# Last output projection's rest as a stream beside the first FFN pair, temporaries' pools swapped, down-weight sums pinned in order, second operand stream reordered

## The chip, the cores and the metric

The kernel runs on one core of a Trainium2 chip. The metric is the device time of one execution in microseconds (us). The engines are PE (TensorE, matrix products), DVE (VectorE), ACT (ScalarE), POOL (GpSimd) and SP (SyncE, which here issues the transfers between HBM and on-chip memory). Each engine works off its own list of instructions in order and waits on semaphores for the others. PE writes its results into PSUM banks; DVE and ACT read them from there.

## The reference

One transformer-like block on a sequence of 2048 tokens of width 1024, in float32. A mixer (attention and mLSTM side by side, then an output projection) adds to the residual stream, and a gated FFN follows. The end of the mixer and the FFN are what matters here:

```python
    mix = merged @ w_out[l]
    x = x + gate_m[:, None, :] * rms_norm(mix, g_post_mix[l])

    h2 = modulate(rms_norm(x, g_pre_ffn[l]), shift_f, scale_f)
    ff = (jax.nn.silu(h2 @ w_ffn_gate[l]) * (h2 @ w_ffn_up[l])) @ w_ffn_down[l]
    x = x + gate_f[:, None, :] * rms_norm(ff, g_post_ffn[l])
```

The FFN's inner width is 2816 = 22 x 128.

## The kernel before

**Products.** A float32 factor is split into a high part (ACT, CAST) and a low part (DVE, the factor less its high part), and a product is three matmuls: high by high, high by low, low by high. Every large matmul is 128x128 by 128x512. In the FFN the split is `split_unit` (L1127 ACT, L1128 DVE), and its tile `hl` lies in a ring of four.

**The mixer** runs over four blocks of 512 tokens. Each block ends with `residual_out` (L514): the output projection in two column halves, four accumulators each. For each of the four token groups of the second half it takes the sum of squares (L524), multiplies by the gate (L526), forms the inverse root (L530, L471, POOL's power L474), scales the first half (L540), loads 2 x 512 columns of the residual x (L553), adds (L538 on DVE, L541 on POOL), stores the new residual (L542) and takes its sum of squares for the FFN's norm (L543, L544). Temporaries `tx` come from a ring of six in the pool `tpool`; `mpool` holds `tm` and the gate vector `gg_m`. Both pools are closed at the end of the mixer, and the FFN's pool `fpool` takes their space.

**The FFN** runs over two token blocks of 1024 (`gate_up(0)`, `down(0)`, `gate_up(1)`, `down(1)`). All three weight products use a Strassen-Winograd scheme: a 2x2 block product as seven products (`PROD`). The weight side of five of them needs sums of weight quarters on DVE (L1295, L1296, L1302). The activation side are seven operands, named 11, 21, T2, T4, T1, T3, 22, that `h_combine` builds: for each of four k-steps it loads four pieces of the residual (L1219), scales them (L1224), transposes them on PE (L210, 4 at a time into a PSUM bank), shifts and scales (L1232), subtracts (L1245, L1255, L1256, L1268) and splits. For the first token block it runs as a stream during the mixer and keeps its results in HBM (`STAGED`, `hc_d`), fetched with L1201; for the second it writes straight into the operand tiles (`PLACED`) while `down(0)` runs.

`gate_up` works through 11 pairs of 256 inner columns. A pair is seven gate products and seven up products of 12 matmuls, four products prepared ahead; `combine` adds them up (L1342 to L1356), the gated results go to HBM (`as_d`), and a_sums (L1395 to L1398) makes four more operands. In `gate_up(0)` each pair also loads its down weights (L1375, into one of nine `big` buffers), makes four sums of them on DVE (L1379 to L1382) and stores them (`ws_d`, L1384). `down` runs the seven products over 11 slices each; at the end of a token group its output is normed (L1463, L1465, L1470), multiplied and added to the residual (L1477) and stored (L1478).

**What sets the order.** The code writes the work down with a clock of estimated matmul times: streams (generators) are due at a time and `tick` steps those that are due between products. In the FFN's runner `run2`, `tick` is called only inside products with `weave` set (those of `down` whose result goes to the "X" bank, 0, 2, 4, 6). After that a scheduler of the framework may move instructions on their engines by its own timing; `tc.keep_in_program_order` forbids this for an instruction.

## Time and profile before

| | |
|---|---|
| median of 3 runs | 2816.28 us (2815.49 to 2817.65) |
| the profiled execution | 2815.8 us; its profile spans 2814.1 us |
| PE busy | 2712.0 us, 96% of the span |
| DVE, ACT, POOL busy | 1936.5, 1241.2, 237.0 us |
| moved by transfers | 417.32 MB |
| last matmul of the mixer, first of the FFN | 1461.3 us from the span's start |
| last product of `down(0)` | 2098.4 to 2140.35 us |
| first pair of `gate_up(1)` | from 2144.4 us |

Times in a profile are microseconds from the span's start, durations of one instruction us or ns as said; "[0.34 <-DMA raw]" at a row's end says that the engine had been idle for 0.34 us before the instruction and what ended it. The granted clock is the share of full speed that PE was given. Buffer numbers are left out there (`hl`, `big`); in rows of the instruction order they stand (`hl_13043`). The views the prediction uses are shown there.

### The profile page before, as it was taken

To read this page: it belongs to the slowest core of one execution; us is meant where nothing else is said; L and a number is where in the kernel's file an instruction comes from. 1 tells how busy PE (TensorE), PEld (TensorE's weight loads), DVE (VectorE), ACT (ScalarE), POOL (GpSimd) and SP (SyncE) were. 2 spreads that over 40 slices of the span, in tenths; PEclk is the share of its full clock that TensorE was granted. 3 is DMA by queue.
4 is the path that set the end of the run, shared out by engine and by line. 5 is a ranking of instruction groups with operands and counts; after the bars stand their busy time and mean duration, and the time that the engine had idled before them with its cause. 6 is when DMAs were issued, how large, how long until landed. Compare 5 with 4: busy or idle time off the path is not lost. (4 is left out here: it accounts for less than half of the span.)

```text
span 2814.1 us, 35152 instructions
## 1 busy us (share of the span) xinstructions
PE 2712.0 (96%) x12654; PEld 2206.6 (78%) x12654; DVE 1936.5 (69%) x3780; ACT 1241.2 (44%) x2278; POOL 237.0 (8%) x255
## 2 busy tenths in 40 slices
PE   6999999999999999999987999999997999999997
PEld 4778888788777888778866888888775888888886
DVE  7768667686776976757647866665668666666556
ACT  4543365433655446554433333334554333333443
POOL 3100120011210112100120000000001000000000
PEclk8999999999999999999998999999998999999999
DMA  7233353243534435334578533235666233234567
GB/s 229 90 109 101 100 180 121 83 132 109 186 118 136 133 126 192 105 116 109 210 264 294 194 107 109 98 105 184 204 204 209 92 110 108 96 108 143 179 201 241
DMA packets 282102, 417.32 MB, mean 148 GB/s; under 512 B 18996, under 2 KB 176312, under 8 KB 280136
## 3 DMA queue, kind: packets, MB, share of 16 engines
q1 hardware_dynamic: 281928, 415.08, 45.5%
q8 instruction: 99, 1.62, 0.2%
q14 instruction: 75, 0.61, 0.1%
HBM read 331.11 MB, written 83.92 MB: 147 GB/s over the span
## 5 line engine op out<-in xcount | busy, mean ns | idle before, releaser
L1127 ACT CAST hl<-raw 128x512 fp32r<-128x512 f32 x528 | 314.6, 621 | 388.9 <-PE mix L205 181.8
L1128 DVE TENSOR_TENSOR hl<-raw,hl 128x512 fp32r<-128x512 f32 x528 | 351.5, 687 | 178.8 <-ACT hl L1127 176.4
L260 ACT CAST whi<-raw 128x1024 fp32r<-128x1024 f32 (+1 forms) x208 | 212.1, 1020 | 412.2 <-PE acc L205 355.5
L261 DVE TENSOR_TENSOR wlo<-raw,whi 128x1024 fp32r<-128x1024 f32 (+1 forms) x208 | 251.7, 1211 | 165.2 <-ACT whi L260 164.6
L205 PE MATMUL acc<-hhi,wlo 128*128 128x512 f32 x896 | 354.2, 395 | 0.0
L205 PE MATMUL acc<-hlo,whi 128*128 128x512 f32 x896 | 352.3, 393 | 0.0
L205 PE MATMUL acc<-hhi,whi 128*128 128x512 f32 x896 | 352.2, 393 | 0.0
L205 PE MATMUL acc<-hl,hl 128*128 128x512 f32 x1056 | 249.7, 394 | 12.9 <-DVE hl L1128 10.9
L205 PE MATMUL acc<-big,hl 128*128 128x512 f32 x1056 | 253.6, 389 | 0.0
L205 PEld LDWEIGHTS acc<-hl,hl 128*128 128x128 f32 x1056 | 197.2, 189 | 60.9 <-DVE hl L1128 17.7
L205 PEld LDWEIGHTS acc<-big,hl 128*128 128x128 f32 x1056 | 198.2, 188 | 41.2
L205 PEld LDWEIGHTS acc<-hlo,whi 128*128 128x128 f32 x896 | 168.3, 188 | 38.7 <-issue 4.1
L205 PEld LDWEIGHTS acc<-hhi,wlo 128*128 128x128 f32 x896 | 168.4, 188 | 37.7 <-issue 3.2
L205 PEld LDWEIGHTS acc<-hhi,whi 128*128 128x128 f32 x896 | 168.4, 188 | 37.5 <-issue 4.1
L205 PE MATMUL mix<-big,hl 128*128 128x512 f32 x704 | 196.6, 391 | 0.3 <-DVE hl L1128 0.3
L205 PE MATMUL mix<-hl,hl 128*128 128x512 f32 x792 | 181.6, 390 | 0.0
L205 PEld LDWEIGHTS mix<-hl,hl 128*128 128x128 f32 x792 | 148.1, 188 | 32.8 <-ACT hl L1127 2.2
L205 PE MATMUL acc<-whi,big 128*128 128x512 f32 x512 | 165.3, 395 | 0.0
L205 PE MATMUL acc<-big,whi 128*128 128x512 f32 x512 | 158.2, 393 | 0.0
L474 POOL TENSOR_TENSOR rs<-ms,nhalf 128x1 f32<-128x1 f32 (+1 forms) x40 | 31.4, 789 | 1471.2 <-DVE ms L471 1433.1
L205 PEld LDWEIGHTS mix<-big,hl 128*128 128x128 f32 x704 | 132.5, 188 | 28.3 <-DVE hl L1128 0.7
L205 PE MATMUL acc<-whi,hhi 128*128 128x512 f32 (+1 forms) x384 | 131.4, 369 | 12.7 <-ACT hhi L506 6.3
(301 smaller groups left out, 4983.4 us busy)
## 6 DMA issues: line engine op xcount, KB each, us to landing
raw<-in_w_in_dram SPq DMA_DIRECT2D x76, 1024.0 KB, 5.3
as_d<-w SPq DMA_DIRECT2D x154, 256.0 KB, 2.1
raw<-as_d SPq DMA_DIRECT2D x70, 512.0 KB, 3.6
raw<-in_w_ffn_gate_dram SPq DMA_DIRECT2D x22, 1024.0 KB, 5.7
raw<-in_w_ffn_up_dram SPq DMA_DIRECT2D x22, 1024.0 KB, 5.3
raw<-ws_d SPq DMA_DIRECT2D x40, 512.0 KB, 5.0
tx<-in_w_ada_dram SPq DMA_DIRECT2D x64, 256.0 KB, 3.6
raw<-in_w_out_dram SPq DMA_DIRECT2D x16, 1024.0 KB, 5.0
```

What stands on the lines that cost most here:

```text
L205: T.matmul(o, lhsT=lhsT, rhs=rhs, start=start, stop=stop, skip_group_check=resumed)
L260: A.copy(hv, src)
L261: eng.tensor_tensor(lv, src, hv.bitcast(F32), op=ALU.subtract)
L474: G.tensor_tensor(r[:, :n], ms[:, :n], nhalf[:, :n], op=ALU.pow)
L1127: A.copy(v(hi), src)
L1128: V.tensor_tensor(v(lo), src, v(hi).bitcast(F32), op=ALU.subtract)
```

## The change

Five things are edited.

1. **The rest of the last output projection becomes four streams.** For block 3 `residual_out` gets a list `late`: the first norm steps stay, the second half's product is kept in a further `big` tile (`keep2`), and scale, load of x, add, store and sum of squares (`norm_and_add`) become generators, started by `open_ffn` and stepped beside the first FFN pair. They load x into the FFN's tiles `w`. The fetch of operand (T3, 0) moves from before the output projection to `rest_of_hc`. The first pair's down weights are loaded only after these streams are finished.
2. **`mpool` and `tpool` change places**, and the FFN's pool gives out a `w` tile before `gg_f`, so that the first `w` tiles lie where `tm` was, not `tx`.
3. **The down weights' load and four sums are kept in program order.**
4. **`h_combine` is written anew**: one load ahead, a fixed order of the four quarters, all four transposed before the differences are formed; steps that take a PSUM bank (`yield gap, True`) run only where `weave` is set, while `tick` is now called in every product of the FFN. For the first token block it starts in block 2 with a gap of 8500 (was: at the end of block 1 plus 20000, gap 9500); for the second its gap is 3000 (was 3800), and it is no longer finished as a whole at the end of `down(0)`: before each of the first gate products of `gate_up(1)` `placed` steps it until that product's operand is complete.
5. A product (`Part`) has a hook `before` for that.

```diff
```diff
@@ -81,8 +81,8 @@
     ps_mix = ctx.enter_context(tc.tile_pool(name="ps_mix", bufs=4, space=PSUM))
+    mpool = p1.enter_context(tc.tile_pool(name="mpool", bufs=1))
     tpool = p1.enter_context(tc.tile_pool(name="tpool", bufs=1))
-    mpool = p1.enter_context(tc.tile_pool(name="mpool", bufs=1))
     opool = ctx.enter_context(tc.tile_pool(name="opool", bufs=1, side="right"))
@@ -210,20 +210,22 @@
     def spawn(gen, delay=0.0):
-        st = [now[0] + delay, gen, False]
+        st = [now[0] + delay, gen, False, False]
         streams.append(st)
...
         try:
-            st[0] = now[0] + next(st[1])
+            r = next(st[1])
+            r, st[3] = r if isinstance(r, tuple) else (r, False)
+            st[0] = now[0] + r
         except StopIteration:
...
-    def tick():
+    def tick(banks=True):
         while True:
-            due = [st for st in streams if st[0] <= now[0]]
+            due = [st for st in streams if st[0] <= now[0] and (banks or not st[3])]
             if not due:
@@ -511,7 +513,7 @@
-    def residual_out(nk, lhs, w, keep, resid, gg, dst, t0):
+    def residual_out(nk, lhs, w, keep, resid, gg, dst, t0, late=None):
@@ -522,10 +524,21 @@
             A.activation(junk, ps, AF.Square, accum_out=ss[:, hf * 4 + t:hf * 4 + t + 1])
-            y = st["keep"][:, t, :] if hf == 0 else tx([P, 512])
+            if late is not None and hf and not t:
+                st["keep2"] = keep([NT, 512])
+            y = st["keep"][:, t, :] if hf == 0 else tx([P, 512]) if late is None else st["keep2"][:, t, :]
             V.tensor_tensor(y, ps, gg[:, hf * 512:(hf + 1) * 512], op=ALU.mult)
...
                 return
+            rest = norm_and_add(t, y)
+            if late is None:
+                for _ in rest:
+                    pass
+            else:
+                late.append(rest)
+
+        def norm_and_add(t, y):
+            ss = st["ss"]
             s = small.tile([P, 1], F32, tag="ss1", name=nm("ss1"), bufs=4)
@@ -533,6 +546,7 @@
                 xr = resid(t, c)
+                yield 4000.0
                 y0 = y if h2 else st["keep"][:, t, :]
@@ -540,6 +554,7 @@
                 nc.sync.dma_start(dst[t * P:(t + 1) * P, c], xr)
+                yield 2000.0
                 A.activation(y0, xr, AF.Square, accum_out=sx[:, h2:h2 + 1])
@@ -549,7 +564,7 @@
         def rows(t, c):
-            xr = tx([P, 512])
+            xr = unit() if "pool" in F else tx([P, 512])
             nc.sync.dma_start(xr, src[t * P:(t + 1) * P, c])
@@ -708,6 +723,8 @@
         yield carry
+        if b == 2:
+            yield lambda: F.update(hc=spawn(h_combine(0, STAGED, 8500.0)))
@@ -1076,17 +1093,16 @@
                 R_ada.append(spawn(ada_stream([(5, "gate")], 12000.0)))
-                R["hc"] = spawn(h_combine(0, STAGED, 9500.0), 20000.0)
-                F["hc"] = R["hc"]
             if b + 1 < NBLK:
...
         if b + 1 == NBLK:
-            yield lambda: [fetch(n_, i_) for n_, i_ in (("T4", 1), ("T1", 0), ("T1", 1), ("T3", 0))]
+            yield lambda: [fetch(n_, i_) for n_, i_ in (("T4", 1), ("T1", 0), ("T1", 1))]
         last = list(residual_out(KD, lambda kk, t: tuple(R[m, kk // 4][:, kk % 4, t * P:(t + 1) * P] for m in ("mh", "ml")),
-                                 a["w_out"][0], big, load_rows(x_d[b * TB:(b + 1) * TB, :]), gg_m, x1[b], b * NT))
+                                 a["w_out"][0], big, load_rows(x_d[b * TB:(b + 1) * TB, :]), gg_m, x1[b], b * NT,
+                                 F["rest"] if b + 1 == NBLK else None))
         yield from last[:-1]
@@ -1109,7 +1125,7 @@
     HC = {}
-    F = {}
+    F = {"rest": []}
     as_d = [tc.dram_tile([P, 7, NP, TB], F32, name=f"as_d{i}") for i in range(NB2)]
@@ -1132,6 +1148,7 @@
             self.raw, self.prep, self.mms, self.weave = raw, prep, mms, weave
+            self.before = lambda: None
             raw.left += 1
@@ -1166,9 +1183,9 @@
             advance()
+            it.before()
             for _ in it.mms(made.pop(done)):
-                if it.weave:
-                    tick()
+                tick(it.weave)
             done += 1
@@ -1211,6 +1228,7 @@
                 split_unit(v, hc_part(name, 0)[:, k, :], hc_part(name, 1)[:, k, :])
+                F["put"].add((name, k))
@@ -1232,46 +1250,45 @@
+        QUADS = ((0, 0), (0, 1), (1, 0), (1, 1))
+        order = [(k, half, i) for k in range(4) for half, i in QUADS]
+        x_ = load(*order[0])
+        yield gap
         for k in range(4):
             q = {}
...
+            for half, i in QUADS:
                 scaled(x_, i)
+                yield gap, True
+                q[f"{half + 1}{i + 1}"] = turned(x_, k, half)
+                if (half, i) != (1, 1):
+                    x_ = load(*order[order.index((k, half, i)) + 1])
+                    yield gap
+            t1 = ob()
+            V.tensor_tensor(t1, q["12"], q["11"], op=ALU.subtract)
+            yield gap
+            put("11", k, q.pop("11"))
+            V.tensor_tensor(q["12"], q["22"], q["12"], op=ALU.subtract)
+            yield gap
             t2 = ob()
+            V.tensor_tensor(t2, q["22"], t1, op=ALU.subtract)
+            put("21", k, q["21"])
             yield gap
+            V.tensor_tensor(q["21"], q["21"], t2, op=ALU.subtract)
+            put("T2", k, t2)
             yield gap
+            put("T4", k, q.pop("21"))
+            if k < 3:
+                x_ = load(k + 1, 0, 0)
             yield gap
+            put("T1", k, t1)
             yield gap
             put("T3", k, q.pop("12"))
             yield gap
             put("22", k, q.pop("22"))
             yield gap
     def rest_of_hc():
+        for n_, i_ in (("T3", 0), ("T3", 1), ("22", 0), ("22", 1)):
             fetch(n_, i_)
@@ -1371,15 +1388,15 @@
         def load():
+            if not p:
+                finish(F["rest"])
             st["raw"] = big([2, D])
-            nc.sync.dma_start(st["raw"], wdn[p * 256:(p + 1) * 256, :].rearrange("(k p) c -> p k c", p=P))
+            tc.keep_in_program_order(nc.sync.dma_start(st["raw"], wdn[p * 256:(p + 1) * 256, :].rearrange("(k p) c -> p k c", p=P)))
...
             q = {f"{k + 1}{h + 1}": st["raw"][:, k, h * TB:(h + 1) * TB] for k in range(2) for h in range(2)}
-            V.tensor_tensor(q["11"], q["12"], q["11"], op=ALU.subtract)
-            V.tensor_tensor(q["12"], q["22"], q["12"], op=ALU.subtract)
-            V.tensor_tensor(q["22"], q["22"], q["11"], op=ALU.subtract)
-            V.tensor_tensor(q["21"], q["21"], q["22"], op=ALU.subtract)
+            for o, x, y in (("11", "12", "11"), ("12", "22", "12"), ("22", "22", "11"), ("21", "21", "22")):
+                tc.keep_in_program_order(V.tensor_tensor(q[o], q[x], q[y], op=ALU.subtract))
             for i, n in enumerate(("11", "22", "12", "21")):
@@ -1415,6 +1432,9 @@
             gp, up = list(pair_parts(wg, p, done_g)), list(pair_parts(wu, p, done_u))
+            if b2 and p == 0:
+                for i, pt in enumerate(gp):
+                    pt.before = lambda i=i: placed(PROD[i][1])
             load, sums = down_weights(p)
@@ -1505,7 +1525,8 @@
             def next_h():
-                F["hp"] = spawn(h_combine(b2 + 1, PLACED, 3800.0), 4000.0)
+                F["put"] = set()
+                F["hp"] = spawn(h_combine(b2 + 1, PLACED, 3000.0))
@@ -1514,14 +1535,20 @@
                     yield make(raw, i, p0 + j, j)
-        if not last:
-            yield lambda: finish([F["hp"]])
+
+    def placed(name):
+        st = F["hp"]
+        while (name, 3) not in F["put"]:
+            now[0] = max(now[0], st[0])
+            step(st)
...
         F["pool"] = ctx.enter_context(tc.tile_pool(name="fpool", bufs=1, reuse_waits="tile"))
+        unit()
         F["gg"] = F["pool"].tile([P, D], F32, name="gg_f")
         nc.sync.dma_start(F["gg"], gg_f_d)
+        F["rest"] = [spawn(r, 1000.0 + i * 4000.0) for i, r in enumerate(F["rest"])]
...
         for i, ch in enumerate(ADA):
```
```

Line numbers rise in the changed file (the split is L1143 and L1144, the weight sums L1312, L1313, L1319, the residual's add L552 and L555, the down weights L1394, L1399, L1401).

**PE at the start of the FFN.** `hc` are operands 11 and 21, hcT2h and hcT4h the high parts of T2 and T4; the first row is the first FFN product after the mixer's last matmul. Before:

```order
L205 MATMUL mix_13150<-hc_12573,hl_12978 128x512 x11
L205 MATMUL acc_13132<-hc_12572,hl_12975 128x512 x12
L205 MATMUL mix_13150<-hc_12573,hl_12978 128x512
L205 MATMUL acc_13132<-hcT2h,hl_13126 128x512
L205 MATMUL acc_13132<-hcT2l,hl_13126 128x512
L205 MATMUL mix_13191<-hcT4h,hl_13129 128x512
```

In the change:

```order
L205 MATMUL mix_13073<-hc_12577,hl_12980 128x512 x11
L205 MATMUL acc_13046<-hc_12576,hl_12977 128x512 x12
L205 MATMUL mix_13073<-hc_12577,hl_12980 128x512
L205 MATMUL mix_13126<-hcT4h,hl_13043 128x512
L205 MATMUL mix_13126<-big_12751,hl_13043 128x512
L205 MATMUL mix_13126<-hcT4h,hl_13043 128x512 x2
```

The product with T4, whose weight side is a plain quarter (hl_13043), now stands ahead of that with T2, whose weight side is a sum; both still follow the first 24 matmuls.

**DVE at the same place.** `raw` are the gate weights, hl_13126 (before) and hl_13040 (change) the low part that the T2 product needs. Before, from the end of the residual's rest:

```order
L544 TENSOR_TENSOR sx_13093<-sx_13093 128x1
L471 TENSOR_SCALAR ms_13106<-sx_13093 128x1
L1379 TENSOR_TENSOR big_13502<-big_13502 128x512
L1380 TENSOR_TENSOR big_13502<-big_13502 128x512
L1295 TENSOR_TENSOR w_13122<-raw_12971 128x512
L1381 TENSOR_TENSOR big_13502<-big_13502 128x512
L1296 TENSOR_TENSOR w_13123<-w_13122,raw_12971 128x512
L1302 TENSOR_TENSOR raw_12971<-raw_12971 128x4x128
L1382 TENSOR_TENSOR big_13502<-big_13502 128x512
L1344 TENSOR_TENSOR w_13145<-mix_13150,w_13145 128x512
L1302 TENSOR_TENSOR raw_12971<-raw_12971,w_13123 128x4x128
L1128 TENSOR_TENSOR hl_13126<-w_13123,hl_13126 128x512
```

In the change, from the last accumulator of the output projection:

```order
L530 TENSOR_TENSOR big_12991<-acc_12892,gg_m 128x512
L543 TENSOR_TENSOR ss_13163<-ss_12853 128x1
L1312 TENSOR_TENSOR w_13036<-raw_12973 128x512
L473 TENSOR_SCALAR ms_13165<-ss_13163 128x1
L1313 TENSOR_TENSOR w_13037<-w_13036,raw_12973 128x512
L1319 TENSOR_TENSOR raw_12973<-raw_12973 128x4x128
L1319 TENSOR_TENSOR raw_12973<-raw_12973,w_13037 128x4x128
L1144 TENSOR_TENSOR hl_13040<-w_13037,hl_13040 128x512
L1144 TENSOR_TENSOR hl_13043<-raw_12973,hl_13043 128x512
```

The residual's adds and the sums of a second set of down weights (big_13502) no longer stand ahead of the weight sums; the adds (L552) come 11 rows or more after these rows.

**SP's queue at the start of the FFN.** Before, from the fourth load of x:

```order
L553 DMA tx_13036<-in_x_dram 128x512
L1201 DMA big_13120<-hc_d 128x2048
L1375 DMA big_13208<-in_w_ffn_down_dram 128x2x1024
L542 DMA x_3_194<-tx_12998 128x512
L542 DMA x_3_194<-tx_13004 128x512
L542 DMA x_3_194<-tx_13036 128x512
L553 DMA tx_13062<-in_x_dram 128x512
L542 DMA x_3_194<-tx_13030 128x512
```

In the change, from the load of the FFN's gate vector on (raw_13124 are the second pair's gate weights):

```order
L1550 DMA gg_f<-gg_f_d 128x1024
L568 DMA w_13060<-in_x_dram 128x512
L568 DMA w_13093<-in_x_dram 128x512
L1382 DMA raw_13124<-in_w_ffn_gate_dram 128x8x256
L568 DMA w_13131<-in_x_dram 128x512
L568 DMA w_13143<-in_x_dram 128x512
L568 DMA w_13159<-in_x_dram 128x512
```

The loads of x go into `w` tiles and have the second pair's gate weights among them. The down weights, of which before four sets are loaded ahead of the second pair's gate weights, come after all stores of the residual, and from there one load and one group of four stores per pair.

**PE at the start of `gate_up(1)`.** `ident,ob` are the transposes of `h_combine`. Before, from the end of `down(0)`:

```order
L210 MATMUL mix_18267<-ident,ob_18262 128x128 x4
L205 MATMUL acc_18338<-hc_12572,hl_18100 128x512 x9
L210 MATMUL mix_18282<-ident,ob_18279 128x128 x4
L205 MATMUL acc_18338<-hc_12572,hl_18100 128x512 x3
L210 MATMUL mix_18292<-ident,ob_18289 128x128 x4
L205 MATMUL acc_18338<-hcT2h,hl_18129 128x512
```

In the change, from the last rows of `down(0)` (hl_18216):

```order
L205 MATMUL acc_16372<-hl_18216,hl_18213 128x512 x2
L205 MATMUL mix_18354<-hc_12577,hl_18224 128x512 x12
L205 MATMUL mix_18399<-hcT4h,hl_18330 128x512
L205 MATMUL mix_18399<-big_12751,hl_18330 128x512
L205 MATMUL acc_18333<-hc_12576,hl_18221 128x512 x12
L205 MATMUL mix_18399<-hcT4h,hl_18330 128x512 x2
L205 MATMUL mix_18399<-big_12751,hl_18330 128x512
```

Before, five of `h_combine`'s 16 groups of four transposes stand here and five in the last product of `down(0)`; in the change four stand in the last product and none here, the other twelve (before: six) in products 0, 2 and 4 of `down(0)`. The first gate products follow the last down product directly.

More of the change, by code (lines that the diff above doesn't have):

```diff
@@ L1233, in turned @@
             return q
+        QUADS = ((0, 0), (0, 1), (1, 0), (1, 1))
+        order = [(k, half, i) for k in range(4) for half, i in QUADS]
+        x_ = load(*order[0])
+        yield gap
         for k in range(4):
             q = {}
-            for half, i, name in ((0, 0, "11"), (0, 1, "12")):
-                x_ = load(k, half, i)
-                yield gap
+            for half, i in QUADS:
                 scaled(x_, i)
-                yield gap
-                q[name] = turned(x_, k, half)
-                yield gap
+                yield gap, True
[9 more added lines that the diff above has]
+            yield gap
             t2 = ob()
-            V.tensor_tensor(t2, q["12"], q["11"], op=ALU.subtract)
-            put("11", k, q.pop("11"))
+            V.tensor_tensor(t2, q["22"], t1, op=ALU.subtract)
+            put("21", k, q["21"])
             yield gap
-            put("T1", k, t2)
-            x_ = load(k, 1, 1)
+            V.tensor_tensor(q["21"], q["21"], t2, op=ALU.subtract)
+            put("T2", k, t2)
             yield gap
-            scaled(x_, 1)
+            put("T4", k, q.pop("21"))
+            if k < 3:
+                x_ = load(k + 1, 0, 0)
             yield gap
-            q["22"] = turned(x_, k, 1)
+            put("T1", k, t1)
             yield gap
-            V.tensor_tensor(t2, q["22"], t2, op=ALU.subtract)
-            V.tensor_tensor(q["12"], q["22"], q["12"], op=ALU.subtract)
             put("T3", k, q.pop("12"))
@@ L1259, in h_combine @@
             put("22", k, q.pop("22"))
-            x_ = load(k, 1, 0)
-            yield gap
-            scaled(x_, 0)
-            put("T2", k, t2)
-            yield gap
-            q21 = turned(x_, k, 1)
-            yield gap
-            put("21", k, q21)
-            V.tensor_tensor(t2, q21, t2, op=ALU.subtract)
-            yield gap
-            put("T4", k, t2)
             yield gap
     def rest_of_hc():
-        for n_, i_ in (("T3", 1), ("22", 0), ("22", 1)):
+        for n_, i_ in (("T3", 0), ("T3", 1), ("22", 0), ("22", 1)):
             fetch(n_, i_)
```

1 line of the change is left out of this document (removed).

## The prediction

> **What bounds the kernel now.** I read the page first (busy shares, then the forty slices), then PE's waits, then busy windows over the stretches where a slice falls short, and last the timeline inside them.
>
> ```profile
> PE 2712.0 (96%) x12654; PEld 2206.6 (78%) x12654; DVE 1936.5 (69%) x3780; ACT 1241.2 (44%) x2278; POOL 237.0 (8%) x255
> PE   6999999999999999999987999999997999999997
> PEclk8999999999999999999998999999998999999999
> ```
>
> PE sets the time: a slice is 70 us, and all are full but the first, the last, and those around 1480 and 2140, where the clock falls too. The change touches just these two inner places: A, from the mixer into the FFN, and B, from `down(0)` into `gate_up(1)`. Windows of the large matmuls alone (length, busy, count, granted clock, transfer share, GB/s):
>
> ```profile
> 1461.31:1560.00 98.69, 71.38 (x296) 0.86 0.91 305
> 1560.00:1900.00 340.00, 340.00 (x1501) 1.00 0.34 114
> 1915.00:2098.00 183.00, 179.65 (x783) 1.00 0.60 198
> 2098.44:2140.35 41.91, 32.98 (x133) 1.00 0.81 267
> 2140.35:2174.94 34.59, 16.69 (x42) 0.65 0.50 171
> 2200.00:2560.00 360.00, 360.00 (x1590) 1.00 0.32 104
> ```
>
> The last row is PE at its best: 360 / 1590 = 0.2265 us a matmul. By that price A (first row) holds 296 x 0.2265 = 67.0 us of work in 98.7: **31.6 us lost**. B is two rows: 133 matmuls, 30.1 us, in 41.9 (11.8 lost, the last product of `down(0)`), and 42, 9.5 us, in 34.6 (25.1 lost, the first pair): **36.9 us lost**. These losses hold idle time, slow clock and, in B, transposes. No more than 68.5 us can be won here.
>
> **A, step by step.**
>
> ```profile
> PE acc L205 <- ACT hl L1127: 23.5, 1, 23.5
> ...
> 1490.42 0.80 PE L205 MATMUL acc<-hcT2h,hl 128*128 128x512 f32 x1 [23.51 <-ACT hl L1127]
> ...
> 1482.42 0.15 DVE L471 TENSOR_SCALAR ms<-sx 128x1 f32<-128x1 f32 x1
> 1486.49 0.69 DVE L1379 TENSOR_TENSOR big<-big 128x512 f32<-128x512 f32 x1 [3.92 <-DMA big<-in_w_ffn_down_dram]
> 1487.83 0.68 DVE L1295 TENSOR_TENSOR w<-raw 128x512 f32<-128x512 f32 x1
> 1488.43 0.69 DVE L1381 TENSOR_TENSOR big<-big 128x512 f32<-128x512 f32 x1
> 1489.03 0.69 DVE L1296 TENSOR_TENSOR w<-w,raw 128x512 f32<-128x512 f32 x1
> ...
> 1489.75 0.62 ACT L1127 CAST hl<-w 128x512 fp32r<-128x512 f32 x1 [7.09 <-DVE w L1296]
> ```
>
> PE does the 24 matmuls of operands 11 and 21 and then stands 23.5 us, from 1466.9, for the cast of the T2 product's weight sum. The sum (L1295, L1296) is late because DVE does it in order behind the residual's rest (to 1482.4) and behind down weights (L1379) that landed at 1486.5. In the change's order neither stands ahead of it: the rest are streams whose adds follow 11 rows later, the down weights are pinned behind them. The pools' swap lets the sum write a `w` tile with no transfer to wait for.
>
> What is left, from t = 1461.31, goes by these durations (DVE instructions of 512 columns start 0.60 apart, see above):
>
> ```profile
> 1464.31 0.60 ACT L524 ACTIVATE tx<-acc 128x512 f32<-128x512 f32 x1
> 1464.81 0.19 ACT L524 ACTIVATION_READ_ACCUMULATOR tx<-acc 128x1 f32 x1
> 1465.83 0.72 ACT L540 ACTIVATE big<-big,rs 128x512 f32<-128x512 f32 x1 [0.84 <-POOL rs L474]
> ...
> 1465.26 0.54 POOL L474 TENSOR_TENSOR rs<-ms,nhalf 128x1 f32<-128x1 f32 x1
> ```
>
> - The last accumulator is done at 0.3 (a matmul shows 0.39 us). On ACT: its sum of squares to 1.1, two scalings to 2.6, the third after DVE's product and small steps (2.9) and POOL's power (3.7, with hand-overs of 0.1 to 0.2) to 4.4, then the casts for T2 and T4 to 5.6; DVE's two low parts to 6.3. PE comes for T4 at 24 x 0.2265 = 5.4 and for its low part 0.5 later: 0.7 us lost.
> - SP loads two of the eight x tiles, then the second pair's gate weights, which wait for the seventh split of the first; that split's ring place is free only after the T2 product, at about 11.6. So six x loads go out from about 13.4, and the adds that need them start on DVE behind the split for up's second product, which waits for a ring place freed by the T1 product (17.1). From there to the low part of up's T4 factor DVE has 16 full instructions, 10 us: 28.3. PE wants it at about 25.7: 2.6 us lost.
>
> That is 3.3 us. On top comes POOL, whose four adds now run beside a full DVE:
>
> ```profile
> 1473.93 1.26 POOL L541 TENSOR_TENSOR tx<-big,tx 128x512 f32<-128x512 f32 x1 [3.76 <-DMA tx<-in_x_dram]
> ...
> 1473.97 1.23 DVE L530 TENSOR_TENSOR ss<-ss 128x1 f32<-128x1 f32 x1
> ...
> 1482.22 0.16 DVE L544 TENSOR_TENSOR sx<-sx 128x1 f32<-128x1 f32 x1 [0.85 <-ACT tx L543]
> ```
>
> A one-column DVE add takes 0.16 us, but 1.23 beside POOL's add: up to 1.1 us for each, 4.4 for four. DVE has waits in this stretch that can take some, so I take 2.7. **A leaves 6.0, wins 25.6.** Bounds: 2 us left if the x tiles are early and POOL falls into waits; 13 if POOL costs its 4.4 and the x loads come later by the landing of 1 MB of weights (5.4 us, rows under B).
>
> The Trainium skill, "SBUF — State Buffer", section "SBUF: two separate sides", says that VectorE with two SBUF inputs and GpSimd take one shared port pair by turns and for a whole instruction. The row of 1.23 us agrees. By that rule the eight powers would count like the adds; it speaks against the change and is the first rival below.
>
> **B, step by step.**
>
> ```profile
> 2098.44:2140.35 41.91, 35.12 (x153) 26.28 (x152) 40.18 (x73) 26.73 (x54) 4.92 (x4) 1.00 0.81 267
> 2099.47 0.60 PE L210 MATMUL mix<-ident,ob 128*128 128x128 f32 x4
> 2125.58 2.73 DVE L1477 SCALAR_TENSOR_TENSOR w<-w,rs,w 128x512 f32<-128x512 f32 x4
> 2133.77 0.38 SPq L1365 DMA_DIRECT2D raw<-in_w_ffn_gate_dram  x1
> 2139.18 0.69 DVE L1295 TENSOR_TENSOR w<-raw 128x512 f32<-128x512 f32 x1 [0.34 <-DMA raw<-in_w_ffn_gate_dram]
> 2144.42 3.31 PE L205 MATMUL acc<-hc,hl 128*128 128x512 f32 x9 [2.29 <-DVE w L1465]
> ```
>
> In the last product DVE is busy 40.2 of 41.9 us (fourth number of the first row), with the splits, the outputs of half the tokens and `h_combine`'s third and fourth step. In the change's order DVE has 67 rows from the product's first additions to its last split: 51 full ones at 0.60, 8 output adds at 0.65 (the x4 row), 8 one-column ones at about 0.1 = 36.6 us; seven `h_combine` rows fewer than before. Starting 2 us before the product, DVE ends at 34.6, and PE's last 8 matmuls need 1.8 more: 36.4 instead of 41.9.
>
> Then the first pair. Its gate weights load once the split before last frees a raw tile, at about 31.2 on that clock, and land 5.4 later (2133.77 to 2139.18) at 36.6. Two casts, 38.1; DVE's lows and sums of that quarter, 39.9; PE's first 12 matmuls end at 42.2. After that I find no wait above 0.5: accumulators are free by 41, the operands of `h_combine` are complete. So 144 matmuls, 32.6 us, end at 42.2: **B leaves 9.6 and wins 27.3**. Off that go the six transposing groups that move into `down(0)`, whose PE is full (third row of the windows): 6 x 0.60 = 3.6. `h_combine` is also denser there (12 groups where 6 were); its steps may be waited for. Of the 5.7 us that stretch now loses (183 less 783 x 0.2265), transposes are 6 x 0.6 = 3.6 and 2.1 is waits for six groups; for six more I take 3. **B wins 20.7.** Bounds of what it leaves and adds: 10 (DVE hides more) to 26 (the output's rows keep holding PE as in 2140 to 2145, and each new group waits 1 us).
>
> **What costs nothing, and its cover.** The down weights' sums: four DVE instructions a pair, 2.4 us, and four stores. A pair of PE lasts 168 x 0.2265 = 38 us, and without them DVE is 69% busy with PE full:
>
> ```profile
> 2200.00:2560.00 360.00, 360.00 (x1590) 298.10 (x1589) 247.22 (x399) 130.12 (x226) 0.00 (x0) 1.00 0.32 104
> ```
>
> So DVE goes to 75%. Uncovered they would cost 11 x 2.4 = 26 us. The earlier start of the staged `h_combine` moves rows in the mixer; there PE loses little, all of it in three places:
>
> ```profile
> 400.00:440.00 40.00, 37.66 (x218) 32.79 (x217) 30.90 (x77) 22.13 (x50) 8.85 (x12) 1.00 0.74 232
> 760.00:800.00 40.00, 36.80 (x208) 32.05 (x207) 31.11 (x88) 20.76 (x43) 7.65 (x10) 0.96 0.69 217
> 1120.00:1180.00 60.00, 57.15 (x339) 48.03 (x338) 42.15 (x112) 33.99 (x79) 8.70 (x11) 1.00 0.34 110
> ```
>
> 2.3, 3.2 and 2.9 us idle. I take no change, with 4 us either way (half of the 8.4).
>
> **Sum.** 2814.1 - 25.6 - 20.7 = 2767.8 us of span. The profiled execution lies 1.7 above its span, and the median of the runs shown 0.5 above that execution: 2767.8 + 2.2 = **2770 us**.
>
> **Rivals.**
> 1. *POOL holds DVE in the first pair for each of its instructions.* Four adds (1.27) and eight powers (0.54) are 9.4 us. For it: the 1.23 us row. Against: ACT and transfers make DVE wait there anyway. Time: A leaves 3.3 + 9.4, 2777 us. This is also what the Trainium skill's port rule gives if every POOL instruction meets a full DVE.
> 2. *The output's tail still binds B.* PE's waits in B that `h_combine` makes are these:
>
> ```profile
> PE mix L210 <- DVE ms L471: 3.2, 1, 3.2
> PE mix L210 <- DVE ob L1224: 2.9, 4, 1.2
> PE acc L205 <- ACT hcT2h L1127: 2.2, 1, 2.2
> PE acc L205 <- DVE hc L1128: 1.8, 1, 1.8
> PE acc L205 <- ACT hc L1127: 1.5, 1, 1.5
> ```
>
>    If only these (11.6) and five transposing groups (3.0) leave the first pair, 10.5 of its 25.1 stay and not 3.3 (9.6 less the last product's 6.3), and if the last product stays at 41.9, another 5.5: 2783 us. For it: the gate weights still wait for a raw tile, DVE keeps its 16 output rows. Against: the count of rows above.
> 3. *The first pair starves instead.* The residual's stores, x loads and the second pair's weights form one queue on SP; were the two loads that PE needs next (gate, then up weights) each late by a landing, 5.4, A would leave 16.8: 2781 us. Against: 13 us of queue stand before a need at 38.
> 4. *The change doesn't do what it says*: the scheduler's order is right but the waits move as a whole, A and B keep their losses: 2816. Nothing in the order speaks for it.
> 5. *Slower: the pinned sums hold DVE.* A sum waits at the head of DVE's queue for its load (the one that landed at 1486.49 was issued at 1479.04, 7.4 us in the crowd), and the next pair's splits stand behind it. It decides once a pair loses more than 46.3 / 11 = 4.2 us; at 7.4 us for each of 11 pairs, 81 us, the time is 2851. Against: the load stands on SP about six products, 16 us, ahead of its sum.
>
> ```profile
> 1479.04 0.38 SPq L1375 DMA_DIRECT2D big<-in_w_ffn_down_dram  x1
> ```
>
> **How the numbers follow.** Forecast 0.52 (its own range 2758 to 2782), rival 1 0.15, rival 2 0.12, rival 3 0.10, rival 4 0.05, rival 5 0.06. Rivals 1 to 3 are faster too, so faster 0.89, same 0.05, slower 0.06, where 0.2% (5.6 us) is what a measurement can tell from no change. The range, 2756 to 2790, takes in the bounds of A and B (best 2814.1 - 29.6 - 26.9 + 2.2 = 2760 and 4 for the mixer; worst -18.6 - 10.9 + 2.2 + 4 = 2791) and leaves out rivals 4 and 5.
>
> **What would show it.** A right: PE's 23.5 us wait for the cast gone, no gap above 3 us and the clock near 1.00 between the mixer's last matmul and the second pair. B right: the last down product near 36 us, no transposes after it, the first pair at full rate within 6 us of it. Down-weight pin right: no DVE wait on L1399 with PE idle behind it. Wrong: a PE wait in A or B above 5 us, or more than 10 us lost in `down(0)` before its last product, or a mixer longer by more than 4 us.

## The result: 2769.5 us where 2770 was forecast, and the profile after

| | before | after |
|---|---|---|
| median | 2816.97 us (2815.49 to 2819.35) | 2769.53 us (2767.92 to 2770.67) |
| ratio | | 0.9835 (95%: 0.9822 to 0.9847) |
| profiled execution, its span | 2815.8, 2814.1 us | 2767.92, 2766.2 us |
| PE, DVE busy | 2712.0, 1936.5 us | 2700.2, 1932.0 us |
| mean granted clock | 0.985 | 0.992 |

The forty slices of the page after (PE's busy tenths, then the granted clock): the falls around 1480 us are gone, and of those around 2140 PE has one tenth left, the clock none.

```profile
PE 2700.2 (98%) x12654; PEld 2204.7 (80%) x12654; DVE 1932.0 (70%) x3780; ACT 1233.8 (45%) x2276; POOL 239.3 (9%) x255
PE   6999999999999999999999999999998999999997
PEclk8999999999999999999999999999999999999999
```

Where the 47.9 us of span went is read best by landmarks: the same matmul is looked up in both traces, and the stretch between two such matmuls is compared. Six stretches follow, windows of the large matmuls alone (length, busy, count, granted clock, transfer share, GB/s): from the mixer's end to the T3 product of the third pair's up weights (A); from there to the last T3 product of `gate_up(0)`, called its end below; from there through `down(0)` up to its last product; the last product; the first pair of `gate_up(1)` up to its first T3 product; from there to the last T3 product. Where products interleave, the landmark is the point at which as many matmuls have begun as in the kernel before. Before:

```profile
1461.31:1599.26 137.95, 110.64 (x469) 0.90 0.80 273
1599.26:1903.90 304.64, 304.64 (x1345) 1.00 0.32 104
1903.90:2098.44 194.54, 190.80 (x830) 1.00 0.60 197
2098.44:2140.35 41.91, 32.98 (x133) 1.00 0.81 267
2140.35:2176.37 36.02, 18.12 (x49) 0.67 0.48 164
2176.37:2576.21 399.84, 399.84 (x1766) 1.00 0.31 102
```

After:

```profile
1460.02:1568.35 108.33, 106.70 (x469) 1.00 0.57 199
1568.35:1872.99 304.64, 304.64 (x1345) 1.00 0.47 159
1872.99:2073.27 200.28, 193.46 (x830) 1.00 0.61 205
2073.27:2111.51 38.24, 33.54 (x133) 0.96 0.81 274
2111.51:2129.22 17.71, 14.13 (x50) 0.81 0.74 267
2129.22:2529.05 399.83, 399.83 (x1765) 1.00 0.31 103
```

| stretch | predicted | measured |
|---|---|---|
| mixer | 0 (4 either way) | -1.3 |
| A, first row | -25.6 | -29.6 |
| rest of `gate_up(0)` | 0 | 0.0 |
| `down(0)` before its last product | +6.6 | +5.7 |
| last product of `down(0)` | -5.5 | -3.7 |
| first pair of `gate_up(1)` | -21.8 | -18.3 |
| `gate_up(1)`, then `down(1)` and the end | 0 | 0.0, -0.7 |
| sum | -46.3 | -47.9 |

So the total was met because two errors of four microseconds cancel, which is luck: A came out 4.0 better than predicted, B (rows three to five of the windows) 4.5 worse. The rest of this document is about these two.

In A one gap of PE above 1 us is left where there was one of 23.5 us, the one predicted at up's T4 factor, with 1.59 us for 2.6. In B a gap is left that the prediction did not have, ahead of the first gate product, with slow matmuls behind it: ten in 4.63 us, 0.46 each. PE's rows of after:

```profile
1487.07 0.73 PE L205 MATMUL mix<-hcT4h,hl 128*128 128x512 f32 x2 [1.59 <-DVE hl L1144]
...
2113.81 0.73 PE L205 MATMUL mix<-hc,hl 128*128 128x512 f32 x2 [2.30 <-ACT hl L1143]
2115.82 4.63 PE L205 MATMUL mix<-hc,hl 128*128 128x512 f32 x10 [1.28 <-DVE hl L1144]
```

### The profile page after: what moved, and what is told of

Read it like the earlier page. It is cut to its first block, busy times and chain, and to the rows that moved or that the text cites. A ratio compares the mean times of both kernels' runs of the same rounds, so it can differ in the third digit from the quotient of the medians.

```text
span 2766.2 us, 35112 instructions
## 1 busy us (share of the span) xinstructions
PE 2700.2 (98%) x12654; PEld 2204.7 (80%) x12654; DVE 1932.0 (70%) x3780; ACT 1233.8 (45%) x2276; POOL 239.3 (9%) x255
## 4 chain that ended last, share of the span: by engine, by line
PE 86%; DVE 7%; DMA 4%; issue 1%; ACT 1%; SPq 0%; POOL 0%; POOLq 0%; DVEq 0%; ACTq 0%
PE acc L205 60%; PE mix L205 24%; PE mix L210 2%; DMA tx<-in_w_ada_dram 1%; DVE hl L1144 1%; DVE tm L427 1%; DMA raw<-as_d 1%; DVE wlo L263 1%; ACT hl L1143 0%; DMA hc_d<-os 0%; DVE wlo L260 0%; DMA ob<-x 0%; DMA tx<-in_x_dram 0%; DMA big<-in_w_ada_dram 0%; DMA raw<-in_w_ffn_down_dram 0%
## 5 line engine op out<-in xcount | busy, mean ns | idle before, releaser
L1143 ACT CAST hl<-raw 128x512 fp32r<-128x512 f32 x528 | 314.5, 621 | 388.5 <-PE mix L205 188.0
L1144 DVE TENSOR_TENSOR hl<-raw,hl 128x512 fp32r<-128x512 f32 x528 | 352.0, 688 | 158.3 <-ACT hl L1143 155.7
L205 PE MATMUL acc<-wlo,hhi 128*128 128x512 f32 (+1 forms) x384 | 138.9, 366 | 2.1 <-DVE wlo L260 1.1
```

The costliest lines, as they stand in the source:

```text
L205: T.matmul(o, lhsT=lhsT, rhs=rhs, start=start, stop=stop, skip_group_check=resumed)
L1143: A.copy(v(hi), src)
L1144: V.tensor_tensor(v(lo), src, v(hi).bitcast(F32), op=ALU.subtract)
```

## The experiments

Each kernel is the change with one thing altered, unless said otherwise. Times are medians; the ratio is to the kernel before on the same chip, with its 95% interval. The end of the mixer, whose instructions are the same in most of them, lay between 1460.0 and 1465.0 us in their profiles; a difference of 2 us is therefore read from landmarks and not from the whole time.

### The residual's rest inside the projection again

```diff
-                                 ..., gg_m, x1[b], b * NT, F["rest"] if b + 1 == NBLK else None))
+                                 ..., gg_m, x1[b], b * NT, None))
```

> The change with the residual's rest (scale, x, add, store, sum of squares) again inside the last output projection; pools' swap, pinned down weights and new h_combine stay. Theory (the rest's adds standing ahead of the T2 product's weight sum on DVE are the larger part of A's loss; the down weight that landed late is worth about 5 us of it): the long PE wait behind the mixer is back at about 19 us, A loses about 24 of its 32 us, 2791 to 2797 us. Rival (the pin alone won A, since in the kernel before the sum came 0.2 us after a down weight's): wait gone or under 6 us, 2769 to 2775 us. Nothing changes in B by either.

Measured: 2789.61 us (0.9907, 0.9892 to 0.9922). The long wait is back, shorter than expected (its place in PE's waits: sum, times, longest):

```profile
PE acc L205 <- ACT hl L1143: 18.7, 4, 15.2
```

DVE does the T2 sum behind the residual's last steps, as before:

```profile
1480.95 0.15 DVE L473 TENSOR_SCALAR ms<-sx 128x1 f32<-128x1 f32 x1
1481.02 0.68 DVE L1312 TENSOR_TENSOR w<-raw 128x512 f32<-128x512 f32 x1
```

The window of A:

```profile
1462.73:1587.07 124.34, 109.16 (x469) 0.93 0.47 158
```

A is 16.0 us longer than in the change (124.34 to 108.33), and loses 18.1 us where 24 were expected; the time lies 1.4 us below the expected range. So the streams are worth 16 of A's 29.6 us where the pin is in place; the pin alone did not win A.

### The pools as before

```diff
-    mpool = p1.enter_context(tc.tile_pool(name="mpool", bufs=1))
     tpool = p1.enter_context(tc.tile_pool(name="tpool", bufs=1))
+    mpool = p1.enter_context(tc.tile_pool(name="mpool", bufs=1))
...
-        unit()
         F["gg"] = F["pool"].tile([P, D], F32, name="gg_f")
```

> The change with mpool and tpool in their former order and without the w tile given out ahead of gg_f. Theory of the prediction (the sum needs a w tile over which no transfer is pending): with the rest as streams no residual is stored from tx any more, so the swap has nothing left to win: 2768 to 2772 us. Rival (the w tiles over tx still wait for the scalings or transfers of the mixer): the T2 sum comes late by 3 us or more and A loses that and as much again by a slower clock: 2775 us or more.

Measured: 2769.65 us (0.9838, 0.9823 to 0.9852), and A to 0.03 us the same:

```profile
1461.35:1569.65 108.30, 106.71 (x469) 1.00 0.57 200
```

The prediction gave the swap a part in A. Beside the streams it has none. The likely reason is that the residual no longer leaves from `tx`, so that no transfer stands over the first `w` tiles either way; this is argued and not shown.

### The down weights free to be moved

```diff
-            tc.keep_in_program_order(nc.sync.dma_start(st["raw"], wdn[...]))
+            nc.sync.dma_start(st["raw"], wdn[...])
...
-                tc.keep_in_program_order(V.tensor_tensor(q[o], q[x], q[y], op=ALU.subtract))
+                V.tensor_tensor(q[o], q[x], q[y], op=ALU.subtract)
```

> The change with the down weights' load and sums free to be moved by the scheduler; all else stays. In its order the loads and sums of later pairs come forward: five pairs' sums stand within the first two to three pairs. Theory (the pin's worth is that it keeps sums whose load may be late off DVE's queue in the crowded first pair): DVE waits for down weights there, PE loses 3 to 10 us between the mixer's end and the fourth pair, 2772 to 2780 us. Rival (the pin did nothing, streams and operands won all): 2768 to 2771 us. Third: the pin cost something in gate_up(0), and without it the time falls below 2767 us.

Measured: 2782.89 us (0.9884, 0.9870 to 0.9899). The time lies above the expected range. From the mixer's end to the end of `gate_up(0)` it takes 9.8 us more than the change (422.72 to 412.97), at the upper edge of what was expected there; of the rest of the difference, 2.8 us stand behind `gate_up(1)`, where nothing was altered. A and the rest of `gate_up(0)`:

```profile
1461.20:1571.71 110.51, 107.75 (x469) 1.00 0.88 308
1571.71:1883.92 312.21, 307.44 (x1345) 0.99 0.36 119
```

Only 2.2 us of it lie in A (110.51 to 108.33) and 7.6 behind it (312.21 to 304.64), most of these at the end of the third pair. There DVE stands 4.81 us ahead of a sum. SP had issued two down-weight loads at 1567.04, behind four stores of earlier sums, and the sum came 4.9 us after them; PE then waits for a split behind it.

```profile
1558.16 3.92 SPq L1401 DMA_DIRECT2D ws_d<-big  x4
1567.04 1.72 SPq L1394 DMA_DIRECT2D big<-in_w_ffn_down_dram  x2
1571.96 0.69 DVE L1399 TENSOR_TENSOR big<-big 128x512 f32<-128x512 f32 x1 [4.81 <-issue]
1575.11 3.54 PE L205 MATMUL mix<-big,hl 128*128 128x512 f32 x10 [2.78 <-DVE hl L1144]
```

The profile names no releaser for the 4.81 us; that it was the landing is read from the two times. This is rival 5's mechanism, a sum that holds DVE for its load, and it works where the pin is missing: in the kernel before, and not in the change.

### The operands as before

```diff
-        QUADS = ((0, 0), (0, 1), (1, 0), (1, 1))
...
+            for half, i, name in ((0, 0, "11"), (0, 1, "12")):
...
-                F["hp"] = spawn(h_combine(b2 + 1, PLACED, 3000.0))
+                F["hp"] = spawn(h_combine(b2 + 1, PLACED, 3800.0), 4000.0)
```

> The change with h_combine as before (its steps, gaps 9500 and 3800, starts, finished as a whole at the end of down(0); its steps run only where weave is set, as before); streams, pools and pin stay. Theory (B was won by h_combine's new order, A by the rest): A stays as in the change (2.4 us lost), B is as in the kernel before, so the time is the change's plus 16 us, with 1 us of the mixer: 2784 to 2789 us. Rival (part of B's loss came from the first part's edits or from the clock): below 2779 or above 2795 us.

Measured: 2787.41 us (0.9896, 0.9880 to 0.9913). From the end of `gate_up(0)` to the first T3 product of `gate_up(1)` it takes 272.39 us, the change 256.23: 16.2 of difference, and the six stretches above gave 16.2 (5.7 - 3.7 - 18.3). The second part of the change is `h_combine` and nothing else.

### The operands alone

The kernel before with the new `h_combine`, that is the change without its streams, its swap and its pin (the first three diffs together).

> The kernel before with the new h_combine, its starts, gaps and hook alone: the residual's rest inside the last output projection, pools as before, down weights free to move. Theory (the edits act in two separate places; B and the denser down(0) belong to h_combine, worth 16 us net, A to the streams and the pin): A loses its 32 us again, the long wait for the T2 product's cast is above 20 us, B as in the change: 2796 to 2803 us. Rival (streams and pin each won the same microseconds twice over, or the new operands changed A too): below 2793 us or above 2806 us.

Measured: 2802.89 us (0.9946, 0.9929 to 0.9962). A is as in the kernel before, in its window and in PE's row:

```profile
1462.72:1601.91 139.19, 110.67 (x469) 0.90 0.78 270
```

```profile
1492.04 0.79 PE L205 MATMUL acc<-hcT2h,hl 128*128 128x512 f32 x1 [23.72 <-ACT hl L1143]
```

To the end of `gate_up(0)` it loses 30.9 us against the change, all of them in A (139.19 to 108.33). Streams off alone cost A 16.0. The other 14.9 appear when the pin and the swap are gone too; pin off alone cost A 2.2, and swap off alone nothing. So this part is lost only where the residual's rest is inside as well. DVE's rows show down-weight sums in front of the T2 sum (L1312), the first of them held 3.44 us by its load:

```profile
1488.06 1.42 DVE L1399 TENSOR_TENSOR big<-big 128x512 f32<-128x512 f32 x2 [3.44 <-DMA big<-in_w_ffn_down_dram]
1489.44 0.69 DVE L1312 TENSOR_TENSOR w<-raw 128x512 f32<-128x512 f32 x1
```

How much of the 14.9 is the pin's and how much the swap's, no run separates.

### The streams' adds on DVE instead of POOL

```diff
-                    G.tensor_tensor(xr, y0, xr, op=ALU.add)
+                    (G if late is None else V).tensor_tensor(xr, y0, xr, op=ALU.add)
```

> The change with the four adds of the streams (L555) on DVE instead of POOL. In the change's trace one DVE instruction beside such an add took 1.78 us instead of 0.68. Theory (DVE's waits in the first pair take what POOL costs; four more DVE instructions, 2.4 us, stand in the row that leads to up's T4 factor): PE's wait for that factor is 1 to 3 us as before, 2767 to 2773 us, no difference that can be told. Rival 1 of the prediction (POOL holds DVE for each of its adds, 1.1 us each, on the path): the factor comes 2 us earlier (4.4 less 2.4), the wait of 1.6 us is gone, 2766 to 2768 us. Third: the adds cost DVE more than POOL did and the wait grows to 4 us or more, 2773 us or more.

Measured: 2771.08 us (0.9834, 0.9819 to 0.9849), no difference in the time; in the trace A is 1.0 us shorter, at full rate but for 1.1 us:

```profile
1463.58:1570.93 107.35, 106.98 (x470) 1.00 0.58 202
```

In the change one of DVE's instructions was stretched beside a POOL add, and nothing more:

```profile
1478.84 1.78 DVE L1412 TENSOR_TENSOR w<-w,w 128x512 f32<-128x512 f32 x1
1478.66 1.41 POOL L555 TENSOR_TENSOR w<-big,w 128x512 f32<-128x512 f32 x1 [0.29 <-DMA w<-in_x_dram]
```

So the four adds cost PE 1.0 us more on POOL than on DVE, which gets four more instructions for it. The prediction had 2.7 us for them, rival 1 had 9.4 for the adds and the powers, which stay on POOL in both kernels.

### A smaller gap, so that the last product has no transposes

```diff
-                F["hp"] = spawn(h_combine(b2 + 1, PLACED, 3000.0))
+                F["hp"] = spawn(h_combine(b2 + 1, PLACED, 1200.0))
```

> The change with a gap of 1200 instead of 3000 for the second h_combine: in its order the transposing groups of down(0) stand seven in its first product, five in the third, four in the fifth and none in the last. Theory (the last product and the first pair are late because DVE, busy 35.8 of 38.2 us there, also does the last k-step's 15 rows, 9 us): the last product falls to 31 to 34 us, the gate weights are asked for as much earlier, PE's wait for them falls under 2 us and the half clock behind it goes; 11 us are won, 1 to 4 given back by denser products before: 2758 to 2765 us. Rival (the output rows and the splits alone hold PE there, the h_combine rows fill waits): last product above 36 us, 2767 to 2773 us. Third (the denser first products lose what the last one wins): 2770 us or more.

Measured: 2772.57 us (0.9841, 0.9827 to 0.9856): no gain. By stretches (`down(0)` before its last product, the last product, the first pair):

```profile
1875.89:2081.03 205.14, 194.50 (x829) 1.00 0.61 205
2081.03:2116.27 35.24, 31.88 (x132) 1.00 0.83 280
2116.27:2130.11 13.84, 11.30 (x49) 1.00 0.75 272
```

The last product wins 3.0 us, of which four transposing groups are 1.4 (in the change one starts at 2090.08 and the next large matmul at 2090.44); the first pair wins 3.9; `down(0)` gives 4.9 back, where those groups now stand and more waits with them. The theory priced DVE's 15 rows at 9 us of PE's time, and at most 1.6 is left for them, the better clock (1.00 for 0.96) included: DVE's backlog in the last product is at its start, where eight additions of the product before and the output rows stand, and that stays. What the first pair shows is worth more: with idle times of 1.26 and 1.28 us instead of 2.30 and 1.28, the clock stays at 1.00.

### The first pair's weights in two halves

```diff
-            nc.sync.dma_start(t, w[:, p * 256:(p + 1) * 256].rearrange("(k p) c -> p k c", p=P))
+            v = w[:, p * 256:(p + 1) * 256].rearrange("(k p) c -> p k c", p=P)
+            for k in ((4, 0) if p == 0 else (0,)):
+                n = 4 if p == 0 else KD
+                nc.sync.dma_start(t[:, k:k + n, :], v[:, k:k + n, :])
```

> The change with the first pair's gate and up weights loaded in two halves each, the half that the first product needs first. Theory (PE's 3.6 us idle ahead of the first gate product, and the 3.4 us of half clock behind it, come from the 6.2 us that 1 MB takes to land): the first half lands about 3 us earlier, the wait falls under 1 us, the clock stays at 1.00, 4 to 7 us are won: 2762 to 2766 us. Rival (the halves share their queues with the output's stores and x loads, and land no earlier, or ACT and DVE are late themselves): 2767 to 2772 us.

Measured: 2769.12 us (0.9834, 0.9819 to 0.9849), no gain. The halves were issued from 2111.18; ACT's first cast of them and DVE's first sum came at 2117.84 and 2117.83, 6.7 us later, as with one load. Whether the first half lay there earlier and ACT's first cast waited for the second, the rows don't tell; so this run says only that halving does not help. The edit also halves the first loads of `gate_up(0)`, and in the profile A is 3.1 us longer than in the change (111.43 to 108.33); that execution was the slowest of the four by 4 us, and whether the halves did it is not shown.

### The operands finished as a whole

```diff
-            if b2 and p == 0:
-                for i, pt in enumerate(gp):
-                    pt.before = lambda i=i: placed(PROD[i][1])
...
+        if not last:
+            yield lambda: finish([F["hp"]])
```

> The change without the hook in front of the first gate products: h_combine is finished as a whole at the end of down(0), as before, with the new order of its steps and the new gap. Theory (B was won by the steps' order; by the end of down(0) all transposes are done, and only splits are left): within 2 us of the change, 2767 to 2773 us. Rival (the hook matters, since otherwise the last operands' splits stand on DVE ahead of the first gate weights' splits and sums, 6 rows of 0.6 us): 3.6 us more wait and a slower clock behind it, 2774 us or more.

Measured: 2772.18 us (0.9839, 0.9823 to 0.9855); from the end of `gate_up(0)` to the first T3 product of `gate_up(1)` 256.43 us, for 256.23 in the change. The hook (edit 5) is worth nothing here: the order of `h_combine`'s steps won B.

### The first gate weights loaded early

Two of the nine `big` tiles are free during `down(0)`; the first pair's gate weights go into one of them instead of a `raw` tile.

```diff
+        def gate_ahead():
+            t = F["gate0"] = big([KD, 256])
+            nc.sync.dma_start(t, wg[:, 0:256].rearrange("(k p) c -> p k c", p=P))
         for i in range(7):
+            if i == 6 and not last:
+                yield gate_ahead
...
         def load():
+            if ahead:
+                return F["gate0"]
```

> The change with the gate weights of the first pair of gate_up(1) loaded early in down(0) into one of the nine big tiles, two of which are free then; nothing else is altered. Theory (the first pair's 7.0 us, 3.6 idle and 3.4 at half clock, come from the weights' landing alone, asked for only when the last but one split frees a raw tile): PE's waits ahead of the first gate product fall under 1 us in sum, no window of the first pair shows a clock below 0.95, 4 to 7 us are won: 2762 to 2766 us. Rival (ACT and DVE, still busy with the output rows, are as late with the first quarter's casts and sums as the weights were): 1 to 3 us won, 2767 to 2769 us. Third (the tile or the early transfer delays the splits of down(0)): 2770 us or more.

Measured: 2766.39 us (0.9820, 0.9806 to 0.9835). PE goes from the last product into the first gate product without a gap, and the first pair runs at full clock. The windows of last product and first pair, and PE's rows:

```profile
2080.43:2118.59 38.16, 33.71 (x134) 0.96 0.81 272
2118.59:2129.74 11.15, 11.01 (x49) 1.00 1.02 361
```

```profile
2108.22 10.37 PE L205 MATMUL acc<-hl,hl 128*128 128x512 f32 x44 [0.48 <-DVE hl L1144]
2118.43 3.32 PE L205 MATMUL mix<-hc,hl 128*128 128x512 f32 x12
```

The first pair is 6.6 us shorter (17.71 to 11.15), all but 0.4 of what it lost. So the late arrival of the weights was its cause, idle time and slow clock together: the issue that waits for a raw tile, and 6.2 us of landing. No wait for ACT or DVE took its place. The median is only 3.1 us under the change's, just outside the expectation. The profiled execution, the slowest of the four, ended its mixer at 1465.0, and its A, which the edit does not touch, is 1.8 us longer than the change's (110.15 to 108.33), with 3.4 us at half clock in it.

### The same with the adds on DVE

The two edits above together.

> The kernel with the early gate weights, and also the four adds of the streams on DVE instead of POOL. In the trace with the adds on DVE alone the wait for up's T4 factor fell from 1.6 to 0.3 us and the first pair was 1.0 us shorter. Theory: 1 us under the kernel with the early weights, 2761 to 2765 us. Rival (that microsecond was chance): no difference from the kernel with the early weights within 2 us.

Measured: 2763.06 us (0.9814, 0.9799 to 0.9828). Its stretches A and first pair take 107.32 and 11.14 us, 1.0 and 6.6 less than the change's, so that both gains show together. The median is 6.5 us under the change's; the intervals of the two ratios overlap, so the times alone do not prove it, the stretches do. It is the best version found.

## Why the prediction was right, and where its steps were wrong

**The place and cause of A** were right. The wait for the T2 product's cast is gone, no gap is above 1.6 us, the clock is 1.00. Of the causes named, the residual's rest is shown by a run (16.0 us of A with the pin in place); that of the down weights ahead of the sum by the row of 3.44 us in the kernel with the operands alone, though its share of the 14.9 us there is not separated from the swap's. The swap won nothing beside the streams; what it would win without them is open. **A's sum was mis-sized by 4.0**: 6.0 left was predicted, and 108.33 less 469 x 0.2265 leaves 2.1, at the lower bound. By the starts of PE's rows the T4 product cost about 0.4 for 0.7 (its rows at 1465.70 and 1466.13 stand 0.43 apart and not 0.23), and up's T4 factor about 1.8, with POOL's part in it, for 2.6 and 2.7. The term that failed most is POOL's 2.7: one DVE instruction was held 1.1 us, and moving the adds won 1.0. Two of the four adds ran while DVE waited.

**The pinned sums cost nothing**: the rest of `gate_up(0)` has 304.64 us at 304.64 busy in both traces. Rival 5 fell for the change, and its mechanism was found in the opposite version.

**`down(0)`** was right in sum, 6.6 predicted and 5.7 measured, but not in its terms. The 0.60 us of a transposing group is the length that its row shows; the next matmul starts after 0.36. So six groups are 2.2 us and not 3.6, and 3.5 of the 5.7 are waits, for 3.

**The last product** was mis-sized by 1.8: 36.4 predicted, 38.24 measured. The count of 67 rows was right, and DVE did end them earlier than before, at 2109.9. That is 36.6 after the product's start, and the step "starting 2 us before the product, DVE ends at 34.6" failed: DVE starts its additions only 0.9 before the product (2073.27), and stands 0.8 us in two waits for POOL's power, which the sum had at nothing. First row, the longer of the waits (the other is 0.38 at 2096.35), last row:

```profile
2072.35 0.69 DVE L1372 TENSOR_TENSOR w<-mix,w 128x512 f32<-128x512 f32 x1
2085.74 1.42 DVE L1497 SCALAR_TENSOR_TENSOR w<-w,rs,w 128x512 f32<-128x512 f32 x2 [0.44 <-POOL rs L476]
2109.24 0.69 DVE L1144 TENSOR_TENSOR big<-ob,hcT4h 128x512 fp32r<-128x512 f32 x1
```

**The first pair** was mis-sized by 3.5, and here a step was missing. Predicted: the load issued at 31.2 on the product's clock, landed at 36.6, twelve matmuls done at 42.2. Measured, in rows of the change (DVE's split that frees the raw tile, SP's issue, DVE's first sum):

```profile
2105.03 1.28 DVE L1144 TENSOR_TENSOR hl<-raw,hl 128x512 fp32r<-128x512 f32 x2
2106.34 0.38 SPq L1382 DMA_DIRECT2D raw<-in_w_ffn_gate_dram  x1
2112.54 0.69 DVE L1312 TENSOR_TENSOR w<-raw 128x512 f32<-128x512 f32 x1 [2.62 <-DMA raw<-in_w_ffn_gate_dram]
```

And its windows with all engines (length, then busy time and count of PE, its weight loads, DVE, ACT and POOL, granted clock, transfer share, GB/s):

```profile
2111.51:2114.00 2.49, 0.19 (x2) 0.19 (x2) 1.42 (x3) 1.38 (x3) 0.00 (x0) 1.00 1.08 367
2114.00:2120.25 6.25, 4.97 (x12) 3.58 (x12) 6.25 (x16) 3.11 (x10) 0.54 (x1) 0.59 0.77 281
```

The issue is at 33.1 (1.9 late, the last product's error), the landing at 39.3 (6.2 for 5.4), and the twelve matmuls end at 47. 3.6 of the 7.0 us lost are idle; the other 3.4 are matmuls at half clock, for which the sum had no term, though before's window of the same place showed 0.65 and the prediction had read it as a loss that would go with the gaps. A gap of 3.6 us cost 7.

**The rivals.** 1 (POOL) had the right row, but its 9.4 us are more than the 2.1 that A lost in all. 2 (the output's tail) fell: with the weights loaded early the same output rows are there, and the first pair loses 0.4 us at most. But one reason that it named for itself, gate weights that still wait for a raw tile, is what the first pair lost. 3 (x loads and weights late in A) and 4 fell. Of the signs announced, "the first pair at full rate within 6 us" failed (8.7), the others held or nearly did; no wait came near the 5 us that would have refuted the reading. One sign was badly set: `down(0)` before its last product loses 12.3 us (200.28 less 830 x 0.2265), above the 10 that were to count against the reading, but it lost 6.5 before, and the 6.6 forecast on top pass the 10 already.

## What to carry to other kernels

Put work that only ends a stage behind the first operands of the next, and pin a sum behind the load that feeds it: on an engine that works in order, either one standing early holds everything behind it, and PE's gap looks like that of a third party. When a stage's first weights wait for a buffer of the stage before, look for another buffer that is free: the gap they leave can be charged twice, once idle and once at half clock. Check a right total stretch by stretch, with the same matmul as a landmark in both traces; here two errors of 4 us were hidden in it.

## What the hardware showed that was not expected

**About 1.8 us of idle time in one window of 3.413 us halve the clock of the next.** In each of the thirteen profiles of this study all changes of the granted clock lie on a raster of 3.413 us, and where the raster stands differs from profile to profile (its first border 0.49 to 2.98 us after the span's start). PE's idle time in one window of this raster goes with the clock of the next. Between the mixer's end and 2740 us, all 38 windows at full clock with 1.81 us idle or more were followed by one at half clock, and all with up to 1.74 us, 4756 of them, by full clock. Out of half clock the next window was full after 0.54 us idle or less (38 windows) and half again from 0.63 us on (32). So a gap that lies in one window can cost more than a longer one that a border divides. PE's row in the change, after 2.15 us, and two windows of the raster (length, busy, count, then the clock):

```profile
2079.68 4.46 PE L205 MATMUL acc<-hl,hl 128*128 128x512 f32 x12 [2.15 <-DVE hl L1144]
```

```profile
2077.55:2080.96 3.41, 1.28 (x5) 1.00 0.48 151
2080.96:2084.38 3.42, 3.42 (x11) 0.50 0.96 327
```

The same in the kernel with the smaller gap for `h_combine`, after 2.37 us, of which 1.59 lie in one window and 0.79 in the next:

```profile
2087.65 8.89 PE L205 MATMUL acc<-hl,hl 128*128 128x512 f32 x36 [2.37 <-DVE hl L1144]
```

```profile
2083.45:2086.86 3.41, 1.82 (x9) 1.00 0.47 156
2086.86:2090.27 3.41, 2.62 (x11) 1.00 0.51 128
```

The first pair's 3.4 us come out of this as well: 2.69 us idle in one window make the next slow, 0.72 us idle in that one keep the third slow (0.50 to 2121.92), and half of two windows is 3.4 us.

```profile
2111.68:2115.10 3.42, 0.73 (x2) 1.00 1.07 371
2115.10:2118.51 3.41, 2.69 (x6) 0.50 0.85 317
```

The Trainium skill, "TensorE: Matmul & The Clock Gate", section "Part 1: The HAM clock gate (the "warmup" mystery)", has the clock fall to half after an idle window of about 3.4 us, in windows that run freely. The raster of 3.413 us agrees with this. That a whole window must be idle does not: 1.81 us of one were enough.
